# Multiplying the pooling branch's maps into its projection weight

## The chip, the core and the metric

One Trainium2 core runs the whole block. The metric is the device time of one execution in microseconds; the time before is the median of three runs. TensorE (PE) multiplies, VectorE (DVE) and ScalarE (ACT) do the elementwise work, GpSimd (POOL) helps a little, and SyncE (SP) issues most of the transfers.

## The reference

2048 frames of 1024 channels go through one residual block in float32. The part that matters here is branch A, the multi-scale pooling:

```
groups = split(u, 4)                       # u: 2048 x 512, four groups of 128 channels
pooled = [trailing_mean_minus_self(g, w) for g, w in zip(groups, (2, 4, 8, 16))]
mixed  = einsum('bsgc,gcd->bsgd', pooled, pool_w)      # one 128 x 128 map per group
mixed  = mixed.reshape(u.shape) * pool_scale           # one factor per channel
A      = mixed @ w_pool_out                            # 512 x 1024
```

Ahead of it stand an RMS norm and one input projection (pool branch, GLU pair, two gates). Behind it A is multiplied with its gate, the convolution branch B with the other, their sum goes through `w_o`, and an MLP of width 4096 follows, each with its norms and residual.

The map of a group, the factors and `w_pool_out` are all linear and nothing stands between them. So `(pooled_g @ pool_w[g] * scale_g) @ w_pool_out[g]` equals `pooled_g @ (pool_w[g] * scale_g @ w_pool_out[g])`.

## The kernel before

Activations lie with channels on the 128 partitions and frames along the row. The 2048 frames are two blocks of 1024, and the phases run in this order: input projection of block one (glu, pool, ga, gb), A of block one, input projection of block two, B and w_o of block one, A of block two, the MLP's up projection, B and w_o of block two, and the rest of the MLP. Names of tiles in the profile are those of the code without their numbers: `A` is branch A's PSUM tile, `mix` the group products' one, `ga` and `gb` the gates'.

Each product is made in float32r from halves: an operand is cast on ScalarE (high half), the rest is subtracted on VectorE (low half), and three matmuls (high x high, high x low, low x high) stand for one. `matmuls` (L262) issues them: twelve for four chunks of 128 rows. Weights go from memory into `wr` (four buffers), and from there to the halves `wh` and `wl` (three buffers each). A weight's low half is stored to memory (`kept`) when block one makes it and loaded again for block two; `flush` (L252) issues those stores a product later.

PSUM holds three tiles of 128 x 1024 for all products (`psum`, L280), so a fourth result waits for the first one's reader.

The pooling runs in the background of the input projection. `pool_steps` (L1079) is a generator that a lane steps after each product. For each group it makes the trailing sums on VectorE, subtracts the frame itself (L1099), splits the result, multiplies it with the group's map (`mix`, 2 x 3 matmuls of 512 columns), scales it on ScalarE (L1114) and stores it as `mxd`. Before A, `fetch` loads `mxd` and splits it again. `branch_a` (L1153) then makes, for each of four weights `w_po[c]` and two halves of the frames, 24 matmuls of 512 columns, and VectorE multiplies the result with the gate `sad`, loaded three results ahead, and stores it as `mad`. The convolution of 31 taps (L991) is a second background task on VectorE.

The order on each engine comes from a scheduler with priorities: what is traced under `tc.high_priority(offset=n)` is pulled ahead by n, and `ordered`/`mark` tie the first matmul of each product behind the product before it, so TensorE keeps the order of the code. All engines and queues then work in that fixed order.

Of the kernel before, what the change touches and what calls it, by code (L numbers as in the profile page):

```python
# [9 lines left out]
F32R = mybir.dt.float32r  # L10
I32 = mybir.dt.int32
AF = mybir.ActivationFunctionType
ALU = mybir.AluOpType
NOSYNC = mybir.DependencyInfo(mybir.DependencyClass.NoSync, mybir.DependencyReason.SCHED_ONLY)

P = 128
D = 1024
SEQ = 2048
T = 512
# [3 lines left out]
CPS = DC // 2  # L23
CW = 512
CC = CW // P
# [7 lines left out]
URGENT = 1500  # L33
# [5 lines left out]
C_PSC = 8  # L39
# [23 lines left out]
def f32(ap):  # L63
    return ap.bitcast(F32)
# [3 lines left out]
def block_kernel(  # L68
# [13 lines left out]
    nc = tc.nc  # L82

    def pool(name, bufs, stack=ctx, **kw):
        return stack.enter_context(tc.tile_pool(name=name, bufs=bufs, **kw))
# [5 lines left out]
    p_wr = pool("pwr", 4)  # L91
    p_ws = pool("pws", 2)
    p_wh = pool("pwh", 3)
    p_wl = pool("pwl", 3)
# [5 lines left out]
    def nm(s):  # L100
        seq[0] += 1
        return f"{s}_{seq[0]}"

    def mk(pl, tag, dt=F32, shape=(P, TB)):
        return pl.tile(list(shape), dt, tag=tag, name=nm(tag))

    def dram(tag, shape=(P, TB), dt=F32):
        return p_dram.tile(list(shape), dt, tag=nm(tag), name=nm(tag))
# [11 lines left out]
    def sub(o, a, b):  # L120
        return nc.vector.tensor_tensor(o, a, b, op=ALU.subtract)  # L121
# [4 lines left out]
    def load(o, src):  # L126
        return nc.sync.dma_start(o, src)

    def aside(o, src):

        return nc.gpsimd.dma_start(o, src)
# [8 lines left out]
    def mark(i):  # L140
        marks[i.ins.engine] = i.ins
        return i

    def ordered(i):

        to = marks.get(mybir.EngineType.PE)
        if to is not None:
            tc.add_manual_dep(i.ins, to.name, NOSYNC, reason="main line")
        return i
# [44 lines left out]
    def clear_halos():  # L194
# [10 lines left out]
    yd, zd, mxd = (  # L205
        {(b, c, p): dram(tag, dt=dt) for b in range(NB) for c in range(CC) for p in parts}
        for tag, dt, parts in (("yd", F32, (0,)), ("zd", F32, (0,)), ("mxd", F32, (0,)))
    )
    fd, lod = {}, {}

    def col(i):
        return cst[:, i : i + 1]


    def split(src, pl, tag):
        hi = mk(pl, tag, F32R)
        lo = mk(pl, tag, F32R)
        nc.scalar.copy(hi, src)
        sub(lo, src, f32(hi))
        return hi, lo  # L220

    def split_w(src, n=TB, low=None, home=None):
        hi = mk(*(home or (p_wh, "wh")), F32R)
        lo = mk(*(home or (p_wl, "wl")), F32R)
        nc.scalar.copy(hi[:, :n], src[:, :n])  # L225
        if low is None:
            sub(lo[:, :n], src[:, :n], f32(hi[:, :n]))
        else:
            load(f32(lo), low)
        return hi, lo  # L230

    ahead = [AHEAD]

    def load_w(src, key):
        with tc.high_priority(offset=ahead[0]):
            raw = mk(p_wr, "wr")
            load(raw, src)
            known = kept.get((key, "low"))
            w = split_w(raw) if known is None else None
            if key is None:  # L240
                return w
        if w is None:
            with tc.high_priority(offset=260):
                w = split_w(raw, low=known)
        if known is None:
            kept[key, "low"] = dram("kept")
            later.append((kept[key, "low"], f32(w[1])))
        return w

    kept, later, due = {}, [], []  # L250
# [10 lines left out]
        order += [(1, k, 0) for k in range(n - 1)]  # L261
        return order + [(0, n - 1, 0), (0, n - 1, 1), (1, n - 1, 0)]  # L262

    def matmuls(ps, w, at, rhs, start=True, stop=True, main=True):

        order = passes(len(rhs))
        for n, (wp, k, xp) in enumerate(order):
            i = nc.tensor.matmul(  # L268
                ps,
                w[wp][:, (at + k) * P : (at + k + 1) * P],  # L270
                rhs[k][xp],
                start=start and n == 0,
                stop=stop and n == len(order) - 1,
                skip_group_check=True,
            )
            if main and n == 0:
                ordered(i)
        return i

    def psum(lab):  # L280
        return ps_mm.tile([P, TB], F32, tag="mm", name=nm(lab))
# [195 lines left out]
    class Plain:  # L477
# [15 lines left out]
        def weight(self, m, t, k):  # L493
            q = 2 * m + k
            low = kept.get((self.key, (1, 2, "21", 4)[q], "low")) if t else None
            with tc.high_priority(offset=URGENT if not t else ahead[0]):
                if q not in self.raw:
                    self.get(q)
                w = split_w(self.raw.pop(q), low=low)
            if not t:  # L500
                kept[self.key, (1, 2, "21", 4)[q], "low"] = o = dram("kept")
                aside(o, f32(w[1]))
            return w
# [261 lines left out]
    BIG, TR = (p_big, "big"), (p_tr, "tr")  # L765
    W = HALO + TB

    def tr(dt=F32):
        return mk(*TR, dt)
# [7 lines left out]
    def window(n=TB):  # L777
        return mk(p_v, "v", F32, (P, n))
# [288 lines left out]
    pw = [p_pw.tile([P, CW], F32R, tag=f"pw{i}", name=f"pw{i}") for i in (0, 1)]  # L1067

    def pool_weight():
        raw = mk(p_wr, "wr")[:, :CW]  # L1070
        load(raw, w_pool)
        nc.scalar.copy(pw[0], raw)
        sub(pw[1], raw, f32(pw[0]))

    def pool_steps(b, alone):

        def get(g):
            s, u = window(W), tr()
            load(s, ud[g][:, b * TB : b * TB + W])  # L1079
            load(u, ud[g][:, HALO + b * TB : HALO + b * TB + TB])  # L1080
            return s, u

        s, u = get(0)
        yield 1
        for g in range(CC):
            w, m = WINDOWS[g], 1
            while m < w:
                lo = HALO - (w - 2 * m)
                s2 = window(W) if alone or m in (2, 8) else mk(p_ss, "r", F32, (P, W))
                add(s2[:, lo:], s[:, lo:], s[:, lo - m : W - m])  # L1090
                s, m = s2, 2 * m
                yield
            if b == 0:
                mul(
                    s[:, HALO : HALO + w],
                    s[:, HALO : HALO + w],
                    cst[:, C_CNT + g * HALO : C_CNT + g * HALO + w],
                )
            nc.vector.scalar_tensor_tensor(  # L1099
                u, s[:, HALO:], 1.0 / w, u, op0=ALU.mult, op1=ALU.subtract  # L1100
            )
            if g + 1 == CC:
                done.add(("windows", b))
            yield 1
            hl = split(u, *TR)
            if g + 1 < CC:
                s, u = get(g + 1)
            yield 2
            ps = psum("mix")
            for t in (0, 1):  # L1110
                h = slice(t * T, (t + 1) * T)
                matmuls(ps[:, h], pw, g, [tuple(p[:, h] for p in hl)], main=False)
            o = tr()
            nc.scalar.activation(o, ps, AF.Copy, scale=col(C_PSC + g))  # L1114
            yield
            load(mxd[b, g, 0], o)
            yield

    def cell_of(d, homes):

# [20 lines left out]
    def half(cells, t):  # L1141
        return [tuple(p[:, t * T : (t + 1) * T] for p in hl) for hl in cells]
# [9 lines left out]
    def branch_a(b, mixed, bg):  # L1152


        def gate_of(k):
            sg = tr()
            with tc.high_priority(offset=150) if b else nullcontext():
                load(sg, sad[(b, *k)])
            return sg

        keys = [(c, t) for c in range(CPS) for t in (0, 1)]
        for (c, t), sg in ahead_by_one(keys, gate_of, 2):
            if t == 0:
                w = load_w(w_po[c], ("po", c))
            ps = psum("A")
            for q in (0, 1):
                i = matmuls(ps[:, q * T : (q + 1) * T], w, CC * q, half(mixed, t))
            mark(i)
            flush()
            with tc.high_priority(offset=URGENT):  # L1170
                mark(mul(sg, ps, sg))
            load(mad[b, c, t], sg)
            bg()
# [496 lines left out]
    mixed = fetch(mxd, 0)  # L1670
# [44 lines left out]
    mixed = fetched  # L1715
    n = [0]
# [151 lines left out]
    c00, c01, c11, u = {}, {}, {}, {}  # L1868
# [370 lines left out]
    coming = got  # L2239
    w = [level_weight(1, LEVEL[0], k) for k in (0, 1)]  # L2240
    here, coming = coming[0], coming[1:]
    for n, p in enumerate(LEVEL):
# [11 lines left out]
        w, here = following, there  # L2254
    HALVES = [(p, n) for p in LEVEL for n in (0, 1)]
    at = next(n for n, job in enumerate(jobs) if job[1] in ALONE)
# [21 lines left out]
    for n, item in enumerate(items[:-SLABS]):  # L2278
        if len(item) == 2:
            p, h = item  # L2280
            if n == at:
                lanes += [Lane(2, fin[0, 1].steps(2), fin[1, 1].steps(2, 0, 6))]
            w = weights.pop(n)
# [12 lines left out]
        s, i, b = item  # L2296
        if item == (1, 3, 0):
            for o in (0, 1):
                t = fo()
# [6 lines left out]
        if n and (i in ALONE or b == 0 or (s, i) == FILL[:2]):  # L2306
            w = [weight_down(i, s, o) for o in (0, 1)]
# [11 lines left out]
    coming = [split_of[n] for n in range(len(items) - SLABS, len(items)) if n in split_of]  # L2319
    end = []  # L2320
    lanes.append(Lane(2, fin[1, 0].first_squares()))
    for n, (s, i, b) in enumerate(END):
# [6 lines left out]
        w = [weight_down(i, n, 1, BIG)] if n == 0 else w + [weight_down(i, n, 1, BIG)]  # L2329
# [73 lines left out]
```

## Time and profile before

| what | value |
|---|---|
| runs | 2156.65, 2156.95, 2162.51 us; median 2156.95 |
| profiled execution, span | 2158.8 us |
| TensorE | 9582 matmuls, busy 99% |
| VectorE, ScalarE | busy 78% and 48% |
| memory traffic | 618 MB, mean 286 GB/s |
| `mix` | 48 matmuls between 200.4 and 536.4 us |
| A of block one | from 300.3 to 344.0 us |
| A of block two | from 756.0 to 801.8 us |

The profile is one execution, taken by the hardware profiler. The page does not give that execution's time apart from its span, from the first to the last instruction. Busy time on TensorE is modelled from the pipeline, so the pace of matmuls is read from the chain of waits in order of time, not from a single row's duration.

### The profile page before, as it was taken

To read this page: it belongs to the slowest core of one execution; us is meant where nothing else is said; L and a number is where in the kernel's file an instruction comes from. 1 tells how busy PE (TensorE), PEld (TensorE's weight loads), DVE (VectorE), ACT (ScalarE), POOL (GpSimd) and SP (SyncE) were. 2 spreads that over 40 slices of the span, in tenths; PEclk is the share of its full clock that TensorE was granted. 3 is DMA by queue.
4 is the path that set the end of the run, shared out by engine and by line. 5 is a ranking of instruction groups with operands and counts; after the bars stand their busy time and mean duration, and the time that the engine had idled before them with its cause. 6 is when DMAs were issued, how large, how long until landed. Compare 5 with 4: busy or idle time off the path is not lost.

```text
span 2158.8 us, 25325 instructions
## 1 busy us (share of the span) xinstructions
PE 2137.7 (99%) x9582; PEld 1770.3 (82%) x9582; DVE 1688.7 (78%) x1655; ACT 1043.9 (48%) x1094; POOL 78.1 (4%) x143
## 2 busy tenths in 40 slices
PE   9999999999999999999999999999999999999997
PEld 7888888888888888888888878888888888888887
DVE  7998789998678999996858795677776657576975
ACT  6434463334543445555644675555663332234761
POOL 1000000000000000000000000000000000120002
PEclk9999999999999999999999999999999999999999
DMA  7688998677997788445787699577798997896967
GB/s 258 237 291 307 336 343 311 226 256 284 335 385 244 249 338 292 181 172 207 269 316 283 231 353 359 208 261 288 267 375 313 346 383 254 334 363 240 303 249 210
DMA packets 173930, 618.40 MB, mean 286 GB/s; under 512 B 19312, under 2 KB 21616, under 8 KB 173808
## 3 DMA queue, kind: packets, MB, share of 16 engines
q1 hardware_dynamic: 143168, 506.44, 64.3%
q0 software_dynamic: 17824, 64.07, 8.4%
q10 hardware_dynamic: 12816, 46.27, 5.5%
q8 instruction: 75, 1.23, 0.2%
q14 instruction: 47, 0.39, 0.1%
HBM read 406.89 MB, written 209.81 MB: 286 GB/s over the span
## 4 chain that ended last, share of the span: by engine, by line
PE 89%; DVE 5%; DMA 4%; issue 1%; ACT 1%; SPq 0%; DVEq 0%; ACTq 0%
PE up L268 26%; PE down L268 21%; PE ga L268 7%; PE gb L268 7%; PE glu L268 6%; PE wo L268 6%; PE B L268 4%; PE rb L268 4%; PE A L268 3%; PE pool L268 3%; DVE y L991 1%; DVE big L121 1%; DVE tr L118 1%; PE rb L577 1%; DMA big<-x1d 1%
## 5 line engine op out<-in xcount | busy, mean ns | idle before, releaser
L268 PE MATMUL up<-big,wh 128*128 128x512 f32 x1792 | 480.9, 390 | 1.4 <-DVE big L121 0.8
L268 PEld LDWEIGHTS up<-big,wh 128*128 128x128 f32 x1792 | 335.8, 188 | 73.0 <-DVE big L121 2.1
L225 ACT CAST wh<-wr 128x1024 fp32r<-128x1024 f32 x196 | 205.9, 1051 | 316.1 <-PE up L268 83.8
L991 DVE SCALAR_TENSOR_TENSOR y<-v,cst,y 128x1024 f32<-128x1024 f32 x240 | 307.1, 1280 | 2.8
L268 PE MATMUL down<-big,wh 128*128 128x512 f32 x872 | 295.0, 389 | 0.0
L268 PE MATMUL up<-big,wl 128*128 128x512 f32 x896 | 276.1, 389 | 0.0
L225 ACT CAST wh<-ws 128x1024 fp32r<-128x1024 f32 x128 | 134.6, 1052 | 262.7 <-DVE ws L121 62.6
L268 PE MATMUL down<-big,wl 128*128 128x512 f32 x688 | 212.1, 389 | 0.0
L268 PE MATMUL down<-tr,wh 128*128 128x512 f32 x504 | 196.2, 389 | 0.5 <-DVE tr L121 0.5
L268 PEld LDWEIGHTS up<-big,wl 128*128 128x128 f32 x896 | 168.1, 188 | 34.8
L268 PEld LDWEIGHTS down<-big,wh 128*128 128x128 f32 x872 | 163.6, 188 | 34.0
L121 DVE TENSOR_TENSOR wl<-ws,wh 128x1024 fp32r<-128x1024 f32 x120 | 146.3, 1220 | 56.2 <-ACT wh L225 56.0
L121 DVE TENSOR_TENSOR wl<-wr,wh 128x1024 fp32r<-128x1024 f32 (+1 forms) x121 | 146.2, 1209 | 29.8 <-ACT wh L225 27.8
L121 DVE TENSOR_TENSOR big<-big,big 128x1024 fp32r<-128x1024 f32 (+1 forms) x108 | 129.5, 1219 | 37.2 <-ACT big L1126 12.9
L121 DVE TENSOR_TENSOR tr<-tr,big 128x1024 fp32r<-128x1024 f32 x94 | 112.8, 1219 | 53.7 <-ACT big L1849 41.0
L268 PEld LDWEIGHTS down<-big,wl 128*128 128x128 f32 x688 | 129.2, 188 | 26.8
L268 PE MATMUL wo<-big,wh 128*128 128x512 f32 x480 | 128.7, 390 | 0.7 <-ACT tr L1367 0.7
L268 PE MATMUL glu<-big,wh 128*128 128x512 f32 x464 | 128.0, 397 | 1.1 <-DVE big L121 0.8
L268 PE MATMUL gb<-big,wh 128*128 128x512 f32 x448 | 120.0, 390 | 0.0
L268 PE MATMUL ga<-big,wh 128*128 128x512 f32 x448 | 119.9, 389 | 0.0
L1849 ACT CAST big<-tr 128x1024 fp32r<-128x1024 f32 x70 | 72.0, 1049 | 98.2 <-DMA tr<-fd 75.0
L268 PEld LDWEIGHTS down<-tr,wh 128*128 128x128 f32 x504 | 94.6, 188 | 20.5 <-DVE tr L121 1.0
(240 smaller groups left out, 3435.0 us busy)
## 6 DMA issues: line engine op xcount, KB each, us to landing
tr<-fd SPq DMA_DIRECT2D x98, 512.0 KB, 7.9
wl<-kept SPq DMA_DIRECT2D x85, 512.0 KB, 5.2
wr<-w_down SPq DMA_DIRECT2D x80, 512.0 KB, 7.1
kept<-wl SPq DMA_DIRECT2D x72, 512.0 KB, 5.9
wr<-w_up SPq DMA_DIRECT2D x64, 512.0 KB, 4.7
wr<-w_in SPq DMA_DIRECT2D x59, 512.0 KB, 5.2
fd<-tr ACTq DMA_DIRECT2D x54, 512.0 KB, 4.2
big<-fd SPq DMA_DIRECT2D x48, 512.0 KB, 7.0
```

The costliest lines, as they stand in the source:

```text
L118: return nc.vector.tensor_tensor(o, a, b, op=ALU.add)
L121: return nc.vector.tensor_tensor(o, a, b, op=ALU.subtract)
L225: nc.scalar.copy(hi[:, :n], src[:, :n])
L268: i = nc.tensor.matmul(ps, w[wp][:, (at + k) * P : (at + k + 1) * P], rhs[k][xp], start=start and n == 0, stop=stop and n == len(order) - ...
L577: nc.tensor.matmul(st[:, at + g : at + g + 1], ss[:, g * P : (g + 1) * P], inv_n, start=start is None or (start and g == 0), stop=stop, sk ...
L991: nc.vector.scalar_tensor_tensor(acc, v[:, k : k + TB], wk, acc, op0=ALU.mult, op1=ALU.add)
L1849: nc.scalar.copy(hi, t)
```

## The change

The maps and the scales are multiplied into the projection weight. `pool_weight` now scales the maps, which arrive transposed, row by row and splits them. `folded(c)` loads and splits `w_po[c]`, makes 12 matmuls of 256 columns into one PSUM tile, evicts that as a high half (copy on ScalarE) and a low half (subtraction on VectorE), and queues both for a store. `folded_again(c)` loads both halves for block two. `branch_a` asks for a weight one `c` ahead. `pool_steps` stores the pooled frames as they are, with no split, product or scaling, and with two background steps fewer for each group. The product of A is the same, except that the chunks of the weight now lie two apart (`step=2`).

```diff
     def pool_weight():
         raw = mk(p_wr, "wr")[:, :CW]
         load(raw, w_pool)
-        nc.scalar.copy(pw[0], raw)
-        sub(pw[1], raw, f32(pw[0]))
+        for g in range(CC):
+            s = slice(g * P, (g + 1) * P)
+            nc.scalar.activation(pw[0][:, s], raw[:, s], AF.Copy, scale=col(C_PSC + g))
+            nc.vector.scalar_tensor_tensor(
+                pw[1][:, s], raw[:, s], col(C_PSC + g), f32(pw[0])[:, s],
+                op0=ALU.mult, op1=ALU.subtract,
+            )
+
+    def folded(c):
+
+        with tc.high_priority(offset=ahead[0]):
+            raw = mk(p_wr, "wr")
+            load(raw, w_po[c])
+            w = split_w(raw)
+        ps = psum("fold")
+        for g in range(CC):
+            for n, (a, b) in enumerate(((0, 0), (0, 1), (1, 0))):
+                i = nc.tensor.matmul(
+                    ps[:, 2 * g * P : 2 * (g + 1) * P],
+                    pw[a][:, g * P : (g + 1) * P],
+                    w[b][:, 2 * g * P : 2 * (g + 1) * P],
+                    start=g % 2 == 0 and n == 0, stop=n == 2, skip_group_check=True,
+                )
+                if g == n == 0:
+                    ordered(i)
+        mark(i)
+        hi, lo = mk(p_wh, "wh", F32R), mk(p_wl, "wl", F32R)
+        with tc.high_priority(offset=URGENT):
+            nc.scalar.copy(hi, ps)
+            sub(lo, ps, f32(hi))
+        for k, part in enumerate((hi, lo)):
+            kept["fold", c, k] = dram("kept")
+            later.append((kept["fold", c, k], f32(part)))
+        return hi, lo
+
+    def folded_again(c):
+
+        with tc.high_priority(offset=ahead[0]):
+            w = mk(p_wh, "wh", F32R), mk(p_wl, "wl", F32R)
+            for k in (0, 1):
+                load(f32(w[k]), kept["fold", c, k])
+        return w
...
             yield 1
-            hl = split(u, *TR)
+            load(mxd[b, g, 0], u)
             if g + 1 < CC:
                 s, u = get(g + 1)
             yield 2
-            ps = psum("mix")
-            for t in (0, 1):
-                h = slice(t * T, (t + 1) * T)
-                matmuls(ps[:, h], pw, g, [tuple(p[:, h] for p in hl)], main=False)
-            o = tr()
-            nc.scalar.activation(o, ps, AF.Copy, scale=col(C_PSC + g))
-            yield
-            load(mxd[b, g, 0], o)
-            yield
...
+        weight = folded_again if b else folded
+        coming = weight(0)
         keys = [(c, t) for c in range(CPS) for t in (0, 1)]
         for (c, t), sg in ahead_by_one(keys, gate_of, 2):
             if t == 0:
-                w = load_w(w_po[c], ("po", c))
+                w = coming
+                if c + 1 < CPS:
+                    coming = weight(c + 1)
             ps = psum("A")
             for q in (0, 1):
-                i = matmuls(ps[:, q * T : (q + 1) * T], w, CC * q, half(mixed, t))
+                i = matmuls(ps[:, q * T : (q + 1) * T], w, q, half(mixed, t), step=2)
```

The change moves instructions on the engines that A waits for. First ScalarE from the last casts of `w_po` to the last gate's sigmoid (`gb_2244`) at the start of A in block one, before:

```order
L225 CAST wh_2758<-wr_2756 128x1024
L960 ACTIVATE tr_2547<-gb_2244 128x1024
L785 ACTIVATE big_2616<-big_2616,cst 128x512
L135 DMA sbd_119<-tr_2547 128x1024
L785 ACTIVATE big_2618<-big_2618,cst 128x512 x2
```

The same place in the change, where `wh_2552` is the high half of fold 0, `wr_2564` the second `w_po` and L785 a scaling of a block-two input:

```order
L785 ACTIVATE big_2627<-big_2627,cst 128x512 x2
L960 ACTIVATE tr_2465<-tr_2465 128x1024
L894 COPY r_1089<-rb_2472 128x512
L135 DMA sbd_116<-tr_2465 128x1024
L218 CAST big_2676<-big_2619 128x1024
L960 ACTIVATE tr_2507<-gb_2212 128x1024
L1100 CAST wh_2552<-fold_2539 128x1024
L225 CAST wh_2566<-wr_2564 128x1024
```

Before, three of the four casts of `w_po` stood ahead of the last sigmoid. Now the second one stands behind the copy of fold 0.

VectorE at that place, from the eviction of the gate product before the last (`gb_2397`), before:

```order
L118 TENSOR_TENSOR tr_2505<-gb_2397,tr_2377 128x1024
L121 TENSOR_TENSOR wl_2679<-wr_2676,wh_2678 128x1024
L991 SCALAR_TENSOR_TENSOR y_2426<-v_2389,cst,y_2426 128x1024
L124 TENSOR_TENSOR big_2614<-big_2614,r_1089 128x1024
L991 SCALAR_TENSOR_TENSOR y_2426<-v_2389,cst,y_2426 128x1024 x2
L121 TENSOR_TENSOR wl_2759<-wr_2756,wh_2758 128x1024
```

And in the change, with `wl_2553` the low half of fold 0 and `wl_2567` that of the second `w_po`:

```order
L118 TENSOR_TENSOR tr_2465<-gb_2358,tr_2347 128x1024
L991 SCALAR_TENSOR_TENSOR y_2279<-v_2240,cst,y_2279 128x1024
L121 TENSOR_TENSOR big_2637<-big_2617,big_2636 128x1024
L991 SCALAR_TENSOR_TENSOR y_2279<-v_2240,cst,y_2279 128x1024
L124 TENSOR_TENSOR big_2623<-big_2623,r_1089 128x1024
L991 SCALAR_TENSOR_TENSOR y_2279<-v_2240,cst,y_2279 128x1024
L121 TENSOR_TENSOR big_2677<-big_2619,big_2676 128x1024
L121 TENSOR_TENSOR wl_2553<-fold_2539,wh_2552 128x1024
L121 TENSOR_TENSOR wl_2567<-wr_2564,wh_2566 128x1024
```

Both low halves now stand behind the same seven operations, one after the other.

SyncE's queue ahead of A in block two, where `kept` and `w_po` feed A's weights, `w_up` those of the MLP and `sad` is the first gate, before:

```order
L127 DMA wl_6001<-kept_2585 128x1024
L127 DMA wr_6333<-w_up 128x1024
L127 DMA wl_6093<-kept_2682 128x1024
L127 DMA wr_6370<-w_up 128x1024
L127 DMA wl_6177<-kept_2762 128x1024
L127 DMA tr_5992<-sad_105 128x1024
```

And in the change:

```order
L127 DMA wh_5975<-kept_2556 128x1024
L127 DMA wl_5976<-kept_2557 128x1024
L127 DMA wh_5985<-kept_2587 128x1024
L127 DMA wl_5986<-kept_2588 128x1024
L127 DMA wh_6075<-kept_2705 128x1024
L127 DMA wl_6076<-kept_2706 128x1024
L127 DMA tr_5979<-sad_105 128x1024
```

Three weights are loaded as pairs of halves there; before, only their low halves came at this place, with two loads for the MLP between them, and the raw `w_po` further ahead.

More of the change, by code (lines that the diff above doesn't have):

```diff
@@ L262, in passes, with matmuls @@
         return order + [(0, n - 1, 0), (0, n - 1, 1), (1, n - 1, 0)]
-    def matmuls(ps, w, at, rhs, start=True, stop=True, main=True):
+    def matmuls(ps, w, at, rhs, start=True, stop=True, main=True, step=1):
         order = passes(len(rhs))
@@ L269, in matmuls @@
                 ps,
-                w[wp][:, (at + k) * P : (at + k + 1) * P],
+                w[wp][:, (at + k * step) * P : (at + k * step + 1) * P],
                 rhs[k][xp],
@@ L2385 @@
         "w_in": octets(g["w_in"], IN_OCTS),
-        "w_pool": g["pool_w"].transpose(1, 0, 2).reshape(P, CW),
-        "w_po": pairs(g["w_pool_out"]).reshape(4, P, D),
+        "w_pool": g["pool_w"].transpose(2, 0, 1).reshape(P, CW),
+        "w_po": pairs(g["w_pool_out"]).transpose(0, 1, 3, 2, 4).reshape(4, P, D),
         "w_co": pairs(g["w_conv_out"]).reshape(4, P, D),
```

## The prediction

> **What bounds the kernel now.** First the page's head, its table of engines and its chain of waits.
>
> ```profile
> span 2158.8 us, 25325 instructions
> PE 2137.7 (99%) x9582; PEld 1770.3 (82%) x9582; DVE 1688.7 (78%) x1655; ACT 1043.9 (48%) x1094; POOL 78.1 (4%) x143
> ...
> PE 89%; DVE 5%; DMA 4%; issue 1%; ACT 1%; SPq 0%; DVEq 0%; ACTq 0%
> ```
>
> TensorE is busy 99% of the span and is 89% of the chain. A modelled busy time can hide short gaps, so next the table of waits, PE's rows alone (15 of them; total, times, longest):
>
> ```profile
> PE down L268 <- DVE big L118: 1.9, 1, 1.9
> PE gb L268 <- DMA wl<-kept: 1.6, 1, 1.6
> PE pool L268 <- DVE tr L118: 1.1, 1, 1.1
> ...
> PE rb L704 <- DVE sp L674: 1.0, 2, 0.5
> ...
> PE rb L712 <- DVE fo L680: 0.2, 1, 0.2
> ```
>
> All 15 together are 12.0 us. TensorE waits for next to nothing, so time is won by fewer matmul columns and lost by any new wait of TensorE. What VectorE, ScalarE or the queues save is worth nothing by itself. Third, the chain in order of time around the place of the change gives the price of one matmul:
>
> ```profile
> 276.85 1.36 PE mix L268 x6
> 278.21 16.33 PE gb L268 x72
> ...
> 300.48 43.52 PE A L268 x192
> 344.00 10.88 PE pool L268 x48
> ```
>
> 1.36/6, 16.33/72 and 43.52/192 are all 227 ns: that is the pace of a 512-column matmul, whatever its tile. (The 389 ns of a single row below includes the pipeline behind it.)
>
> **What is removed.** The group products `mix`, of both blocks:
>
> ```profile
> L268 PE MATMUL mix<-tr,pw x48: 389/389/396, 200.4 to 536.4; 128*128 128x512 f32 x48
> ```
>
> 48 x 0.2267 = **-10.9 us** on TensorE. The eight casts, eight subtractions and eight scalings around them go from ScalarE and VectorE too. TensorE waited for none of them, so I price them at nothing.
>
> **What is added on TensorE.** Four folds of 12 matmuls, 48 in all, of 256 columns. The kernel's last products have that shape, each with a weight load of its own, as a fold has:
>
> ```profile
> 2138.96 5.75 PE down L268 x48
> ```
>
> ```profile
> L268 PE MATMUL down<-big,big 128*128 128x256 f32 x128 | 23.9, 285 | 1.9 <-DVE big L118 1.9
> ```
>
> 5.75/48 = 120 ns, so the folds are **+5.8 us**. Matmuls alone would give -5.1 us. The A products themselves stay, 192 matmuls per block.
>
> **What waits now.** Folds 0 and 1 stand together on TensorE, between the last gate product and the first A. In ScalarE's order (shown above) the copy of fold 0 stands ahead of the cast of the second w_po, and on VectorE likewise the two low halves. Fold 1 needs that cast and that low half. So fold 1 waits until fold 0 has been evicted. The hand-offs, from the timelines of ScalarE and VectorE:
>
> ```profile
> 301.86 1.03 ACT L225 CAST wh<-wr 128x1024 fp32r<-128x1024 f32 x1
> 302.80 1.01 ACT L960 ACTIVATE tr<-gb 128x1024 f32<-128x1024 f32 x1
> ...
> 333.79 1.05 ACT L218 CAST big<-tr 128x1024 fp32r<-128x1024 f32 x1 [9.75 <-DVE tr L121]
> ```
>
> ```profile
> 296.64 1.21 DVE L118 TENSOR_TENSOR tr<-gb,tr 128x1024 f32<-128x1024 f32 x1
> 297.78 1.21 DVE L121 TENSOR_TENSOR wl<-wr,wh 128x1024 fp32r<-128x1024 f32 x1
> 298.91 1.28 DVE L991 SCALAR_TENSOR_TENSOR y<-v,cst,y 128x1024 f32<-128x1024 f32 x1
> 300.11 1.22 DVE L124 TENSOR_TENSOR big<-big,r 128x1024 f32<-128x1024 f32 x1
> ...
> 334.87 1.23 DVE L121 TENSOR_TENSOR big<-tr,big 128x1024 fp32r<-128x1024 f32 x1 [1.12 <-ACT big L218]
> ...
> 354.97 1.23 DVE L118 TENSOR_TENSOR tr<-pool,tr 128x1024 f32<-128x1024 f32 x1 [1.37 <-PE pool L268]
> ```
>
> A pool product ended at 344.00 + 10.88 = 354.88 and its reader began 0.09 later; a cast ended at 334.84 and its reader began 0.03 later. One 1024-wide ScalarE operation follows another after 0.94 us; on VectorE it is 1.14, behind a convolution step 1.20. No row shows an eviction into a weight tile; I take the same rates, as the gate's row, which reads a product too, takes no longer than the cast from SBUF. With 0 at fold 0's start:
>
> - fold 0 issues until 1.44 and ends at 1.32 + 0.28 = 1.60
> - its copy runs 1.69 to 2.74; the cast of the second w_po starts at 2.63 and ends at 3.68
> - low half of fold 0 from 2.77, of the second w_po from 3.91 to 5.13
> - fold 1's first matmul at 3.77, the other 11 from 5.2 to 6.5; the first A at 6.5
>
> Without a wait A would start at 2.88. The wait is **3.6 us** if VectorE is free at 2.77. Is it? The gate product before the last ended at 278.21 + 16.33 = 294.54, and its eviction began at 296.64, 2.1 late. In the new order that eviction, three convolution steps and three others, 8.2 us, stand ahead of fold 0's low half, and the eviction can begin 5.9 before fold 0. On time, VectorE is free at 2.3; 2.1 late, at 4.4, and the wait is 5.2. I take the middle: **+4.4 us** (3.6 to 5.2). Below 3.6 it gets only if ScalarE and VectorE run in another order, which they can't.
>
> Folds 2 and 3 I price at nothing: their operands are due when fold 1's are evicted, and 48 A matmuls, 10.9 us, lie between. If that cover went, each would cost the same 3.6.
>
> **The clock.** A gap in TensorE's stream has a second price. Stretches of the windows view (PE's count in brackets, the granted clock behind POOL):
>
> ```profile
> 44.00:46.00 2.00, 1.15 (x4) 0.37 (x2) 1.65 (x2) 1.71 (x3) 0.00 (x0) 1.00 0.76 211
> 46.00:48.00 2.00, 1.37 (x6) 1.01 (x6) 2.00 (x4) 0.00 (x0) 0.00 (x0) 0.90 0.96 387
> 48.00:50.00 2.00, 2.00 (x6) 1.61 (x5) 2.00 (x4) 1.66 (x2) 0.00 (x0) 0.50 0.98 295
> 50.00:52.00 2.00, 2.00 (x8) 1.54 (x8) 2.00 (x3) 0.45 (x1) 0.00 (x0) 0.75 0.38 156
> ```
>
> ```profile
> 2130.95 0.39 PE L268 MATMUL down<-big,big 128*128 128x256 f32 x1 [1.93 <-DVE big L118]
> ```
>
> ```profile
> 2132.00:2134.00 2.00, 2.00 (x20) 2.00 (x18) 2.00 (x3) 0.45 (x2) 1.34 (x2) 1.00 0.00 0
> ```
>
> Four matmuls in 2 us, where nine fit, were followed by a clock of a half: 2 x (0.10 + 0.50 + 0.25) = 1.7 us lost. A plain gap of 1.93 us was not. The new gap, 3.6 to 5.2 with one matmul in it, is longer than either, so I add **+1.7 us**, with 0 as the other end.
>
> The Trainium skill, "TensorE: Matmul & The Clock Gate", section "Part 1: The HAM clock gate", says that the clock halves after an idle window of about 3.4 us and comes back after a busy one, and that the window runs free of the kernel. By it the price is half of 3.4, an estimate of 1.7, or nothing where the gap falls across two windows; the rows agree with the 1.7. It speaks against this change, because the change makes a gap of that length.
>
> **Queues.** Four more stores of 0.5 MB (the high halves) fall on the A stretch, and block two's high halves are loaded where before w_po was:
>
> ```profile
> 300.30:343.80 43.50, 43.50 (x193) 36.05 (x192) 38.85 (x34) 22.60 (x28) 0.00 (x0) 1.00 0.97 360
> ```
>
> At 360 GB/s a store is 1.5 us of transfer, 6 in all, in a stretch that is nearly full (0.97). But the stretch grows by 5.8 + 4.4 + 1.7 = 11.9 us, so I price them at nothing (uncovered, up to 6). What stands behind them on SP's queue are the stores of A's results and later gates, needed 20 us later. In block two each A weight is now two late loads rather than one:
>
> ```profile
> wl<-kept SPq DMA_DIRECT2D x85, 512.0 KB, 5.2
> ```
>
> ```profile
> 756.03 7.01 DMA tr<-sad
> ...
> 779.96 21.83 PE A L268 x96
> ```
>
> A load takes 5.2 us; buffers come free one w_o product (10.9 us) or more ahead of use. The gates `sad` get one more load ahead of them, 1.5 us, and land 8.5 after A's start rather than 7.0. The fourth A result needs the first one's PSUM 16.3 us after the start, so that is covered. The pool weight's four slices, at most four times one 128x512 operation on each engine, run under gate products that wait for none of them (uncovered, at most 4 x 0.7 us).
>
> **Sum:** -10.9 + 5.8 + 4.4 + 1.7 = **+1.0 us**. The reordering of everything else could undo or add waits like the 1.6, 1.1 and 0.5 above: 3 us either way, 0 taken. The profiled span, 2158.8, lies 1.9 over the runs' median of 2156.95; put on the median, the forecast is **2158.0 us**, no change that can be told (a measurement of this kernel tells some 0.3%, 6.5 us).
>
> **Rivals.**
>
> *The gap is cheap.* VectorE is on time and the clock holds: -10.9 + 5.8 + 3.6 = -1.5, and with -3 from waits that vanish -4.5: 2152.5 to 2155.5. For it: the 1.93 us gap that left the clock alone. Against: this one is twice as long.
>
> *An input load holds the fold (slower).* ScalarE runs in order, and two rows of scaling a block-two input stand six rows ahead of fold 0's copy. Before, such a load held ScalarE for 6.2 us just here:
>
> ```profile
> 314.56 1.34 ACT L785 ACTIVATE big<-big,cst 128x512 f32<-128x512 f32 x2 [6.22 <-DMA big<-xt]
> ```
>
> Behind the scaling stand two sigmoids, a short copy and a cast, so it decides once that load lands later than 1.69 - 1.34 - 0.94 - 0.57 - 0.94 - 0.94 = 3 us before fold 0 starts. As late as there, the copy slips 6.2 us: 3.6 + 6.2 in place of 4.4, 1.0 + 5.4 = +6.4, with a late VectorE +8.0: 2163.4 to 2165. For it: DMA at 0.97. Against: in the new order the gates' loads stand behind that load and not ahead of it, so it is issued some 10 us before fold 0.
>
> *The full gain and more.* Some of folds' wait is covered and the 3.2 us of waits above vanish with the casts and subtractions: -5.1 - 3.2 = -8.3, 2148.6. Against: ScalarE's order forbids the first part.
>
> That the products aren't really gone is excluded: TensorE's order has 48 `mix` rows fewer and 48 `fold` rows.
>
> **How the numbers follow.** Forecast 0.50, its own range 2154 to 2162 (wait 3.6 to 5.2, clock 0 or 1.7, 3 us of reordering). Cheap gap 0.27, late input 0.13, full gain 0.05, anything else 0.05. The range 2152 to 2164 holds the first two and half of the third. Faster by over 0.3%: 0.05 + 0.02 = 0.07. Slower: most of 0.13 and what else could stall, 0.15. Within: 0.78.
>
> **What would show it.** Right: `mix` gone, 48 `fold` matmuls at 120 ns; a PE wait at the second fold on ScalarE and then VectorE, 3.6 to 5.2 us, none at folds 2 and 3; a granted clock near 0.5 for some 3 us in the first A; A in block two without a wait on a load. Wrong: that wait under 1 us, a wait on `big<-xt` on ScalarE ahead of fold 0's copy, PE waits on wh or wl loads near the second A, or a difference beyond 6.5 us either way.

## The result, and the profile after

The changed kernel takes **2176.19 us** (median of 5 runs, 2174.99 to 2179.03), the kernel before 2159.93 us beside it (5 runs, 2156.65 to 2164.74). The ratio is **1.0080, 95% interval 1.0065 to 1.0095**: slower, and outside the range I gave. The profiled execution's span is 2173.2 us, against 2158.8.

The head of its page:

```profile
span 2173.2 us, 25288 instructions
PE 2138.6 (98%) x9582; PEld 1770.7 (81%) x9582; DVE 1685.0 (78%) x1654; ACT 1029.4 (47%) x1081; POOL 78.1 (4%) x143
...
PE 84%; DVE 9%; DMA 4%; issue 2%; ACT 1%; SPq 0%; DVEq 0%; ACTq 0%
```

As many matmuls as before, 48 of them shorter, and yet 14.4 us more. In the chain TensorE has lost 5 of its 89 points and VectorE has won 4. So TensorE waits, and its rows in the table of waits (total, times, longest) say for what:

```profile
PE gb L268 <- ACT tr L439: 6.8, 1, 6.8
PE down L268 <- DVE big L118: 2.3, 1, 2.3
PE fold L1089 <- ACT wh L225: 2.0, 1, 2.0
PE pool L268 <- DVE tr L118: 1.8, 1, 1.8
...
PE fold L1089 <- DVE wl L121: 1.1, 1, 1.1
...
PE rb L577 <- DVE sm L118: 1.0, 1, 1.0
```

The 21 rows are 25.6 us together, where the 15 of before were 12.0. The two `fold` rows were foreseen. The largest was not: once, in a gate product of block one, TensorE waits 6.8 us for ScalarE. Stretches of the windows view around it (us, busy time and count of PE, PEld, DVE, ACT, POOL, then the granted clock, the DMA share and GB/s), before:

```profile
270.00:280.00 10.00, 10.00 (x46) 8.29 (x45) 6.20 (x17) 4.25 (x4) 0.00 (x0) 1.00 0.93 318
280.00:290.00 10.00, 10.00 (x46) 8.29 (x45) 8.81 (x9) 6.21 (x7) 0.00 (x0) 1.00 1.00 341
```

and after:

```profile
270.00:280.00 10.00, 6.55 (x29) 5.07 (x28) 9.21 (x16) 4.01 (x5) 0.00 (x0) 1.00 1.03 418
280.00:290.00 10.00, 6.63 (x19) 5.31 (x20) 10.00 (x12) 7.41 (x11) 0.00 (x0) 0.66 0.95 317
```

PE's count falls from 46 to 29 and 19, and the clock that was granted in the second stretch is 0.66. TensorE's timeline after shows both prices, and the wait of the folds that was predicted:

```profile
276.16 0.39 PE L268 MATMUL gb<-big,wl 128*128 128x512 f32 x1
283.37 2.93 PE L268 MATMUL gb<-big,wh 128*128 128x512 f32 x6 [6.82 <-ACT tr L439]
286.09 1.49 PE L268 MATMUL gb<-big,wl 128*128 128x512 f32 x3
...
306.34 0.38 PE L1089 MATMUL fold<-wh,pw 128*128 128x256 f32 x1 [2.05 <-ACT wh L225]
307.84 0.38 PE L1089 MATMUL fold<-wl,pw 128*128 128x256 f32 x1 [1.12 <-DVE wl L121]
...
309.52 2.76 PE L268 MATMUL A<-big,wh 128*128 128x512 f32 x6
```

Six matmuls take 1.52 us at the full clock. After the gate wait they take 2.93, and the two rows 283.37 and 286.09 lie 2.72 apart for six matmuls that need 1.36. All twelve up to 288.55, where the old pace is back, take 5.2 us instead of 2.7: the clock costs 2.5.

Two rows of A, one for each block, give the milestones (matmuls with the weight's high half `wh`; the times are the first and the last start; block two begins at 755.5, not at the 756.0 of the table ahead of the change), of before:

```profile
L268 PE MATMUL A<-big,wh x128: 389/389/389, 300.3 to 343.4; 128*128 128x512 f32 x128
L268 PE MATMUL A<-big,wh x64: 387/389/486, 755.5 to 800.9; 128*128 128x512 f32 x64
```

and of after:

```profile
L268 PE MATMUL A<-big,wh x128: 387/389/628, 309.5 to 356.9; 128*128 128x512 f32 x128
L268 PE MATMUL A<-big,wh x64: 387/389/486, 768.0 to 812.8; 128*128 128x512 f32 x64
```

From these the 14.4 us by stage (a wait counted as what the next start slips):

| up to | before | after | difference | made of |
|---|---|---|---|---|
| first A, block one | 300.3 | 309.5 | +9.2 | opening 1.6 sooner (see below); `mix` -5.4; gate wait +7.0; half clock behind it +2.5; folds 0 and 1 +2.9; from fold 0 to A 6.82 instead of 2.88, +3.9 |
| last A, block one | 343.4 | 356.9 | +13.5 | folds 2 and 3 +2.9; half clock in the first A +1.3 |
| first A, block two | 755.5 | 768.0 | +12.5 | `mix` -5.4; new small waits (pool +0.7, two `rb` +1.6) and a clock of 0.83 from 560 to 570 us, +1.7; 0.4 not accounted for |
| end | 2158.8 | 2173.2 | +14.4 | two waits of `up` +2.1; two waits of before gone (`wo` 0.7, `rb` 0.5), -1.2; the wait of `down` near the end +0.4, and a clock of 0.83 in the 10 us around it, +1.7; 1.1 less than these add up to, not accounted for |

The 1.6 at the opening does not go with the change. Behind nearly the same wait (0.47 and 0.45 us at 28 us) the granted clock of 30 to 40 us was 0.83 in the profiled execution of before and 1.00 in that of after. Of the fourteen profiled kernels four show this fall (0.79 from 28 to 36 us), the kernel before and three versions of the changed one (e5, e10 and e11 below). Without it the two spans would lie 16.0 us apart, as the medians do (16.3).

So the matmuls came out as worked out, and new waits with the clock behind them took more than the gain. Where the largest comes from, ScalarE's timeline shows, before:

```profile
276.89 1.01 ACT L439 COPY tr<-gb 128x1024 f32<-128x1024 f32 x1 [3.12 <-PE gb L268]
278.25 1.12 ACT L1114 ACTIVATE tr<-mix,cst 128x1024 f32<-128x1024 f32 x1 [0.35 <-PE mix L268]
280.71 1.05 ACT L225 CAST wh<-ws 128x1024 fp32r<-128x1024 f32 x1 [1.35 <-DVE ws L121]
...
285.32 2.95 ACT L1126 CAST big<-big 128x1024 fp32r<-128x1024 f32 x3
```

and after:

```profile
274.53 1.05 ACT L1157 CAST big<-big 128x1024 fp32r<-128x1024 f32 x1 [4.04 <-DMA big<-mxd]
275.79 1.05 ACT L1157 CAST big<-big 128x1024 fp32r<-128x1024 f32 x1 [0.21 <-DMA big<-mxd]
278.58 1.05 ACT L225 CAST wh<-ws 128x1024 fp32r<-128x1024 f32 x1 [1.74 <-DVE s L624]
279.53 1.04 ACT L225 CAST wh<-wr 128x1024 fp32r<-128x1024 f32 x1
280.48 1.94 ACT L785 ACTIVATE big<-big,cst 128x512 f32<-128x512 f32 x3
282.32 1.90 ACT L439 COPY tr<-gb 128x1024 f32<-128x1024 f32 x2
```

The copy `tr<-gb` (L439) reads out a gate sum, to which the product after next adds in PSUM. Before, it stood first and ran 0.2 after its product had ended (276.69), one product and a `mix` ahead of need. After, its product ended at 270.94, and TensorE needed the copy at 276.4, after one more product; it ran at 282.32, together with the next one. Ahead of it stood the casts of the pooled tensor (L1157), of which the third waited 4.04 us for its load, two weight casts, of which the first waited, and three scalings of block two's input. What the weight cast waited for stands on SP's queue and on VectorE, after:

```profile
259.05 1.20 SPq L127 DMA_DIRECT2D v<-vd  x1
...
264.66 1.23 SPq L127 DMA_DIRECT2D big<-mxd  x2
266.81 0.32 SPq L127 DMA_DIRECT2D kept<-ws  x1
...
270.69 0.97 SPq L127 DMA_DIRECT2D big<-xt  x2
```

```profile
277.26 1.23 DVE L121 TENSOR_TENSOR ws<-wr,ws 128x1024 f32<-128x1024 f32 x1 [0.79 <-DMA kept<-ws]
```

(The cast's own row names `s`, the short VectorE operation right behind this one.) A buffer of `ws` must first be stored; the store, issued at 266.81 behind loads of `mxd` and `v`, releases VectorE only at 277.26, some 10 us later. On SP's queue before:

```profile
274.31 0.61 SPq L127 DMA_DIRECT2D v<-vd  x1
...
284.05 0.32 SPq L127 DMA_DIRECT2D big<-mxd  x1
...
288.46 0.38 SPq L127 DMA_DIRECT2D big<-xt  x1
```

The convolution's `v` comes 15 us sooner than before, the last `mxd` 19 us and the first `xt` 18 us. So the theory to be tested is: **the pooling lane has become faster, and the loads, casts and convolution steps that follow it have moved into the last gate products, ahead of what TensorE needs.** The rivals: only ScalarE's order there matters; the missing TensorE work makes it; the folds make it; the transfers bound that stretch in any order.

### The profile page after: what moved, and what is told of

The parts are those of the page before. It is cut to its first block, busy times and chain, and to the rows that moved or that the text cites. A ratio compares the mean times of both kernels' runs of the same rounds, so it can differ in the third digit from the quotient of the medians.

```text
span 2173.2 us, 25288 instructions
## 1 busy us (share of the span) xinstructions
PE 2138.6 (98%) x9582; PEld 1770.7 (81%) x9582; DVE 1685.0 (78%) x1654; ACT 1029.4 (47%) x1081; POOL 78.1 (4%) x143
## 4 chain that ended last, share of the span: by engine, by line
PE 84%; DVE 9%; DMA 4%; issue 2%; ACT 1%; SPq 0%; DVEq 0%; ACTq 0%
PE up L268 25%; PE down L268 21%; PE wo L268 8%; PE gb L268 5%; PE glu L268 5%; PE A L268 4%; PE rb L268 4%; PE B L268 4%; PE ga L268 4%; DVE y L991 3%; PE pool L268 3%; DVE tr L118 1%; DVE wl L121 1%; DMA kept<-ws 1%; DVE big L121 1%
```

## The experiments

Times are medians, ratios stand against the kernel before on the same chip. Three chips were used, and the kernel before took 2160.24 us beside e1 to e4, 2159.13 beside e5 to e8, 2159.02 beside e9 to e11 and 2155.50 beside e12; so a difference between two experiments of different groups is good to some microseconds only. The names `e1` to `e12` are used below.

**e1: the gate copies ahead of the casts again.**

```diff
         def run(self, i, then, bg):
-            w, cells = self.w.pop(i, None) or self.weight(i), self.parts.need(i)
+            with behind_copy() if self.first_gb and i in (3, 4) else nullcontext():
+                w = self.w.pop(i, None) or self.weight(i)
+            cells = self.parts.need(i)
 ...
-    branch_a(0, mixed, parts.step)
+    branch_a(0, mixed, step_behind)
```

(`behind_copy` ties ScalarE's new instructions behind the last gate copy; `step_behind` is `parts.step` under it.)

> Edit: on ScalarE the two copies of the gate products (gb) stand ahead of the casts of the last sum weight and of the input scalings again, as they did in the kernel before; nothing else is changed. Theory (ScalarE's queue in order: the copy was late because the cast ahead of it waited for a store): TensorE's 6.8 us wait for a copy at 276 to 283 us shrinks to under 1 us, the granted clock of 280 to 290 us goes from 0.66 to 1.00 (2.2 us), the fold's waits stay: 2167 us, 9 under the changed kernel. Rival (the transfers: the weight behind that store comes no earlier, so TensorE stops as long one product later): 2174 to 2176 us.

Measured: 2174.25 us, 1.0074 (1.0059 to 1.0089). PE's rows in the table of waits of this run:

```profile
PE fold L1102 <- ACT wh L235: 3.9, 1, 3.9
PE fold L1102 <- DVE wl L121: 3.4, 1, 3.4
PE gb L278 <- ACT tr L450: 2.8, 1, 2.8
PE gb L278 <- DVE wl L121: 2.1, 1, 2.1
```

The gate wait shrinks from 6.8 to 2.8, since the copy still stands behind the pooled tensor's casts, one of which waits 5.24 us for its load. But the next weight then comes 2.1 late, and the folds' two waits grow to 7.3, because VectorE works without a pause from 280 to 310 us. The stall moves on: the order on ScalarE is a link of the chain, not its cause. The rival's time was right, and its mechanism in part: TensorE does stop again, but for 2.1 us at the next product and for the rest at the folds.

**e2: fold 1's raw weight in tiles of its own.**

```diff
-            w = split_w(raw)
+            w = split_w(raw, home=BIG if c == 1 else None)
```

> Edit: the two halves of the second raw output weight lie in two tiles of the large pool, so that their cast no longer waits for a weight buffer that fold 0 frees; the gate copies are left behind the cast. Theory (fold 1 waits for a cast that stands behind fold 0's copy): the two waits at fold 1 (2.05 and 1.12 us) go, product A starts at most 5 us after fold 0 instead of 6.8, the clock of the first A product stays at 1.00: 2 to 3.5 us less, 2172.7 to 2174 us; the 6.8 us wait in the gate stays. Rival (A waits for fold 0's low half anyway): A starts 6.5 to 7 us after fold 0 and the time stays at 2176.

Measured: 2171.40 us, 1.0062 (1.0047 to 1.0077), 4.8 less than the changed kernel. TensorE no longer waits at fold 1, and A starts 2.88 us after fold 0 (304.88 to 307.76) instead of 6.82, although the gate wait grew:

```profile
PE gb L268 <- ACT tr L439: 9.6, 1, 9.6
```

So the folds' hand-over was worth 3.9 us on TensorE and about 4.8 by the medians, and it hung on the weight buffer.

**e3: both edits,** e1's and

```diff
-            w = split_w(raw)
+            w = split_w(raw, home=BIG if c == 1 else None)
```

> Edit: both: copies first, and own tiles for the second raw weight. Theory: the savings add, 11 to 12.5 us, 2163.7 to 2165 us; still 4 to 5 above the kernel before, because the waits later on (pool, second block's gate, expansion, the end: 6 us together in the profiled spans) are another cause and stay. Rival (those later waits follow from the lateness of the first block): 2158 us.

Measured: 2175.29 us, 1.0074 (1.0059 to 1.0089): they don't add. TensorE waits 2.6 for the copy, then 4.2 for the next weight's low half.

**e4: the removal without the folds.**

```diff
-        weight = folded_again if b else folded
+        def weight(c):
+            return load_w(w_po[c], ("po", c))
```

> Leaves out the group product: the group products are removed as in the change, but the folds are left out too, and the output weight is loaded, cast and kept as in the kernel before. Its ScalarE order has the cast ahead of the copies as the changed kernel has. Theory (the stall in the gate comes from the removal of the group products, by the order of ScalarE's queue, and not from the folds): the 6.8 us wait and the clock loss are there, the folds' 5.8 + 3.2 + 1.3 us are gone: 2166 us, slower than the kernel before although 10.9 us of TensorE's work are gone. Rival (the folds and their loads bring the stall): 2149 us.

Measured: 2162.76 us, 1.0013 (1.0002 to 1.0024). The wait stands there without any fold, and the clock behind it (waits, then windows, of this run):

```profile
PE gb L268 <- ACT tr L439: 8.0, 1, 8.0
```

```profile
280.00:290.00 10.00, 5.95 (x15) 4.70 (x16) 10.00 (x14) 7.92 (x12) 0.00 (x0) 0.53 0.92 290
```

This kernel leaves out the group product and takes as long as the kernel before, though 10.9 us of matmuls are gone. The removal makes the stall; the folds don't.

**e5: the lane's old pace.** The change had taken two steps a group out of `pool_steps`, with the work that stood between them.

```diff
             yield 1
-            load(mxd[b, g, 0], u)
+            mixed_in = u
             if g + 1 < CC:
                 s, u = get(g + 1)
             yield 2
+            yield
+            load(mxd[b, g, 0], mixed_in)
+            yield
```

> Edit: the changed kernel, but the pooling lane keeps the number of steps a group that it had with the group product: the group's result is stored to mxd two steps later, the next group's loads are issued before it, as in the kernel before; the work is the changed kernel's. By this the orders of ScalarE, VectorE and the transfer queue in the last gate products are close to the kernel before again (mixed tensor's last load, convolution input and casts later, gate copies ahead of them). Theory (the removal sped up the lane, and its transfers, casts and convolution came into the last gate products): the gate wait of 6.8 us and the clock loss of 2.2 go, the fold's waits stay: 2167 us. Rival (TensorE has 5.4 us less work in a stretch that transfers at a share of 1.0 bound whatever the order, as the run with the copies first suggests): 2174 us or more.

Measured: 2166.05 us, 1.0037 (1.0021 to 1.0053), 10 less than the changed kernel, with the same work. In block one's gate TensorE waits 0.7 us, once; the largest wait is now the folds' (this execution is 7 us over the median, so I read its order and not its sum):

```profile
PE fold L1089 <- ACT wh L225: 4.3, 1, 4.3
```

**e6: the old pace, and own tiles for fold 1** (the edits of e5 and e2).

```diff
-            w = split_w(raw)
+            w = split_w(raw, home=BIG if c == 1 else None)
 ...
-            load(mxd[b, g, 0], u)
+            mixed_in = u
 ...
+            yield
+            load(mxd[b, g, 0], mixed_in)
+            yield
```

> Edit: the lane's old pace, and own tiles for the second raw output weight. Theory: 2176.2 less 9 less the 4.8 that the own tiles gave: 2162 to 2163 us, about the kernel before; what is left above 2155 are the waits after the fold. Rival (transfer bound): 2170 us.

Measured: **2158.84 us, 1.0001 (0.9990 to 1.0013)**: the kernel before's time. Both large waits are gone; the longest left is

```profile
PE rb L577 <- DVE sm L118: 2.1, 1, 2.1
```

**e7: the old pace, no folds** (the edits of e5 and e4).

```diff
-            load(mxd[b, g, 0], u)
+            mixed_in = u
 ...
+            yield
+            load(mxd[b, g, 0], mixed_in)
+            yield
 ...
-        weight = folded_again if b else folded
+        def weight(c):
+            return load_w(w_po[c], ("po", c))
```

> Leaves out the group product, and has no folds: the removal alone at the lane's old pace. Theory: the removal alone gave 2162.8 with the faster lane, of which 8.0 us are the gate wait and some 4 the clock; without them 2151 us, the 10 us under the kernel before that the removed matmuls weigh. Rival (transfer bound): 2160 us or more.

Measured: **2151.62 us, 0.9969 (0.9954 to 0.9985)**. The removal alone, at the old pace, is worth 7.5 us of the 10.9; the profiled execution still waits 2.6 us for VectorE at a gate product, which the kernel before does not. Against e4 the pace is worth 11.1 by the medians and 9.5 by the ratios. And against e6 the folds, without a wait, cost 7.2, for 5.8 of matmuls, a difference within the intervals.

**e8: the kernel before with a fast lane.**

```diff
             hl = split(u, *TR)
-            if g + 1 < CC:
-                s, u = get(g + 1)
-            yield 2
             ps = psum("mix")
 ...
-            yield
             load(mxd[b, g, 0], o)
-            yield
+            if g + 1 < CC:
+                s, u = get(g + 1)
+            yield 2
```

> Edit: the kernel before, all of its work kept, with the steps of a group's product drawn together, so that the lane moves as fast as the changed kernel's; ScalarE's queue then has casts of the mixed tensor and the sum weight and an input scaling ahead of the gate copies, as the changed kernel has. Theory (the lane's pace makes the stall, not the folds and not the missing TensorE work): a gate wait of 4 to 8 us appears and the time rises to 2166 to 2170 us. Rival (the missing work makes it: with the group products in place TensorE is late enough): no wait, 2158 to 2161 us.

Measured: 2190.63 us, 1.0150 (1.0132 to 1.0168). The gate wait appears (6.0 us), but so do 9.1 us in which the group products wait for their own split, which I had not counted. So it shows less than it should, and e12 repeats it in a clean form.

**e9: e6 with block one's mean-square sums a step later.**

```diff
-        yield lag
+        yield lag if b else 2
```

> Edit: the run with the lane's old pace and own tiles, and block one's mean-square sums (rb from sm, in the second block's gate) placed one step later in the lane. Theory (TensorE's wait of 2.1 us there and the half clock in the 10 us behind it are the price of a sum placed one product too early): 3 to 4 us less, 2155 us; faster than the kernel before by 0.15 to 0.2 per cent, at the edge of what can be told. Rival (the sum is late because VectorE is behind, so the wait moves with it): 2158 to 2159 us.

Measured: 2159.12 us, 1.0001 (0.9989 to 1.0014). The wait at `rb<-sm` went, and two others came in its place (`gb` for VectorE 2.3, for ScalarE 2.6 in two). The rival was right: no gain.

**e10: e6 without keeping the folded weight.**

```diff
-        for k, part in enumerate((hi, lo)):
-            kept["fold", c, k] = dram("kept")
-            later.append((kept["fold", c, k], f32(part)))
+        for k in (0, 1):
+            kept["fold", c, k] = [d for n, d in kept.items() if n[-1] == "low"][2 * c + k]
```

> Leaves out keeping the folded weight: the eight halves are not stored, and the second block loads the same number of bytes of other stored halves in their place. Otherwise the run with the lane's old pace and own tiles. Theory (the stores, 4 MB in a stretch at a transfer share of 0.8 to 1.0, are hidden behind the products): 2158 to 2159 us, no change. Rival (they delay the loads of the next stage): 2153 us or less.

Measured: 2160.48 us, 1.0009 (1.0000 to 1.0018): no gain, so the stores cost nothing that this shows.

**e11: the gap at the fold filled.**

```diff
         ps = psum("fold")
+        if c == 0:
+            spare = root_psum().rearrange("p (g q) -> p g q", g=G)
 ...
         mark(i)
+        if c == 0:
+            for _ in range(8):
+                mark(ordered(nc.tensor.matmul(
+                    spare, ones, ones.unsqueeze(1).to_broadcast([P, G, P]), start=True, stop=True,
+                )))
```

> Edit: the changed kernel with eight matmuls of ones into a spare bank between fold 0 and fold 1, which fill most of TensorE's wait there; their result is not used. Theory (the half clock of the first A product comes from the gap before it): the first six matmuls of A take 1.52 us again, not 2.76, the wait is 1.8 us shorter on paper and A starts no earlier; 1 to 1.5 us less in all, too little for one time. Rival (the clock drops for another reason): 2.7 us again.

Measured: one time, 2173.67 us, which decides nothing. In the trace the filled part of the gap is gone, the other is not:

```profile
308.39 0.39 PE L1091 MATMUL fold<-wh,pw 128*128 128x256 f32 x1 [0.22 <-ACT wh L225]
310.45 0.58 PE L1091 MATMUL fold<-wl,pw 128*128 128x256 f32 x1 [1.67 <-DVE wl L121]
...
312.96 1.93 PE L268 MATMUL A<-big,wh 128*128 128x512 f32 x6
```

The clock drops all the same, sooner, in fold 1, and is back within the first A (1.93 for six, not 2.76). The wait of 1.67 us with one short matmul ahead of it was followed by a fall, and neither theory foresaw the form.

**e12: the kernel before with two lane steps a group less.** All its work is kept.

```diff
             nc.scalar.activation(o, ps, AF.Copy, scale=col(C_PSC + g))
-            yield
             load(mxd[b, g, 0], o)
-            yield
```

> Edit: the kernel before with two bare lane steps a group taken out (those around the store of the product); split and product stay apart, all work is kept. It is the clean form of the run with the fast lane, in which the group products themselves waited 9.1 us for their split. By its order ScalarE has the casts of the mixed tensor and the sum weight and two input scalings ahead of the last two gate copies, as in the changed kernel. Theory (the lane's pace makes the gate wait, with the group products in place and without folds): no new waits at the group products, a gate wait of 4 to 8 us with a clock loss of 2 us: 2165 to 2169 us. Rival (it needs TensorE to be early, which the removed work made it): under 1.5 us of wait, 2158 to 2161 us.

Measured: **2179.44 us, 1.0100 (1.0078 to 1.0122)**. ScalarE's timeline of this run, and TensorE's:

```profile
281.91 1.04 ACT L225 CAST wh<-ws 128x1024 fp32r<-128x1024 f32 x1 [2.31 <-DVE s L624]
282.86 1.04 ACT L225 CAST wh<-wr 128x1024 fp32r<-128x1024 f32 x1
283.81 1.94 ACT L785 ACTIVATE big<-big,cst 128x512 f32<-128x512 f32 x3
285.66 1.90 ACT L439 COPY tr<-gb 128x1024 f32<-128x1024 f32 x2
```

```profile
286.70 2.93 PE L268 MATMUL gb<-big,wh 128*128 128x512 f32 x6 [5.92 <-ACT tr L439]
```

It is the changed kernel's picture, the same seven instructions in the same order, in the kernel before: no fold, no missing matmul, only two empty steps less in the background task. That settles it. The time came out 10 over what I expected; block two is hurt too (waits of 2.1 at `pool`, 1.7 and 1.8 at two `rb`, 3.1 in two at `up`).

Of the rivals, the folds are out by e4, the missing TensorE work by e12, and the transfers by e5, which moves the changed kernel's data for the same matmuls and takes 10 us less. That only ScalarE's order matters is out by e1, where the stall moved on.

A version that beats both did not come of it: e6 equals the kernel before, and with every wait of the change gone -10.9 + 5.8 leaves 5 us. That is 0.24%, twice what e6's interval leaves open to either side (0.12%), so it would have shown; what takes it up in e6 no run isolates.

## Why the prediction was wrong, step by step

- **`mix` removed, -10.9:** right as work (48 matmuls are gone). As time only 7.5 us at best (e7).
- **Folds, +5.8:** right. The chain gives 1.43 us for 12, 119 ns each; without a wait they cost 7.2 in all (e6 against e7).
- **Wait at fold 1, +4.4 (3.6 to 5.2):** right in place, kind and about in size. A starts 6.82 us after fold 0 (302.70 to 309.52) where I had 6.5 to 8.1, and 2.88 without a wait; so the wait costs 3.9 by the same count. Folds 2 and 3 wait for nothing, as said. e2 shows that the buffer makes it.
- **Clock, +1.7:** right that it falls; 1.3 us here (six A matmuls 2.76 for 1.52). But I counted one gap. It fell at the gate wait (2.5), in block two (1.7) and at the end (1.7) as well. The Trainium skill, "TensorE: Matmul & The Clock Gate", section "Why this matters for your kernels", warns of idle gaps above some 3 us. In these traces some shorter ones did it (last section).
- **Queues, 0:** right for the stores (e10), and block two's A waits for no load.
- **"The reordering of everything else could undo or add waits like the 1.6, 1.1 and 0.5 above: 3 us either way, 0 taken":** this step failed. With the other terms as measured the sum is -10.9 + 5.8 + 3.9 + 1.3 = +0.1; nearly all of the 14.4 us is reordering. I priced it by the waits that the kernel had, all under 2 us, and so took the waits of an order that fitted for those of any order. The removed casts, subtractions and scalings I priced "at nothing", since TensorE waited for none: true of their work, but each group also lost two steps of the lane, and these set when the convolution, the casts of `mxd` and the loads of `xt` come. The text on the change names these two steps; I never priced them. e12 prices them alone, at 1.0% or some 22 us in the kernel before; e5 gives 10 back in the changed one.
- **The rival "an input load holds the fold":** near the mechanism and wrong in place. ScalarE's order did hold TensorE behind scalings of block two's input, but 20 us earlier, at the gate copies, where I read only the fold's neighbourhood. Those scalings waited for no load of their own; what held ScalarE were a load of `mxd` (4.04) and the weight cast (1.74). That the rival's price, 6.2, lies near the 6.8 is chance. I gave it 0.13. A copy whose product ended at 270.94 ran at 282.32, behind work that TensorE did not need yet. The Trainium skill, "TensorE: Matmul & The Clock Gate", section "Architectural detail: the array is 16× 32×32, not 1× 128×128", says that ScalarE and VectorE take their queues strictly in order. These rows agree with it.
- **Range and chances:** every case but one changed the fold's surroundings only, so the range was as narrow as that one place.

## What to carry to other kernels

When a change takes work out of a background task whose steps set the order of other things, compare the whole order around it, on each engine, and look for what has moved *ahead* of the instructions that TensorE waits for: here two empty steps a group were worth more than all the matmuls removed. Keep the steps when the work goes (e5), and only then see whether the faster pace pays. A wait cured at one link of an in-order chain (e1, e9) moves to the next; cure what made the work come early.

## What the runs showed of the hardware

The clock fell after shorter gaps than I had expected, but not after each of them. A wait of 2.14 us at a `pool` product (e12) was followed by six matmuls in 2.38 us instead of 1.52, one of 1.84 at the same place (e2) by a granted clock of 0.68 in the next 4 us, and one of 2.29 at the end of the changed kernel by a mean clock of 0.83. Waits of 1.93 (before), 2.04 (e3), 2.14 again (e12, at `up`), 2.64 (e3, at the gate) and 2.85 us (e1, at the gate) were followed by none. The longest of these, where the 1.66 us for six matmuls include a start from rest and the clock stayed at 1.00:

```profile
278.91 1.66 PE L278 MATMUL gb<-big,wh 128*128 128x512 f32 x6 [2.85 <-ACT tr L450]
```

All waits of 3.25 us and more in these runs, from 3.25 in e8 to 9.6 in e2, had a clock well under 1 behind them (0.50 to 0.64 in the next 4 us). Where one matmul or sixteen one-column matmuls stood beside the gap, 1.67 (e11) and 0.97 us (the changed kernel at `rb<-sm`, 3 us after another of 1.53) were followed by a fall too, as was 0.47 us with sixteen narrow matmuls behind it at the opening of the kernel before. Each fall in the changed kernel cost 1.3 to 2.5 us. So the length of a gap alone does not decide between some 1.8 and 2.9 us. What does, these runs don't settle.
